# The last multiply-add of a conditioning set in PSUM writes the sum to SBUF, in place of a copy by ScalarE

## The chip, the core and the metric

The kernel runs on one core of a Trainium2 chip. The core has a matrix engine (TensorE, PE in the profile; its weight loads are PEld), a vector engine (VectorE, DVE), a scalar engine (ScalarE, ACT), a general engine (GpSimd, POOL) and a sync engine that issues most transfers (SyncE, SP). Each works through its own queue in order; they meet at semaphores. Data lies in SBUF; PSUM is the memory in which TensorE leaves its results. The metric is the device time of one execution in microseconds (us), the median of several runs.

## The reference

A trunk of two layers on 256 tokens of width 2048, in float32. Every sub-layer is normalized, scaled and shifted by a conditioning vector `mod`, and gated by it before the residual add. `mod` is what the change is about:

```python
c_act = jax.nn.silu(c)                       # c: 1 x 2048
for i in range(DEPTH):                       # 2 layers
    mod = c_act @ ada_w[i] + ada_b[i]        # ada_w[i]: 2048 x 12288
    sh1, sc1, g1, sh2, sc2, g2 = jnp.split(mod, N_MOD, axis=-1)
    h = modulate(rms_norm(x, norm_mix_g[i]), sh1, sc1)
    y = token_mixer(h)                       # layer 0: spatial gating; layer 1: attention
    x = x + g1[:, None, :] * y
    h = modulate(rms_norm(x, norm_ffn_g[i]), sh2, sc2)
    x = x + g2[:, None, :] * swiglu_ffn(h, ffn_w_gate[i], ffn_w_up[i], ffn_w_down[i])
return rms_norm(x, final_g)
```

## The kernel before

**Projections.** The large matrix products read weights in chunks of 1 MB (`wchunk`, L301): a load by SP into one of five `raw` buffers (L303), then for each half of the chunk a cast on ACT to a rounded `hi` (L290) and the remainder `lo` on DVE, for some chunks on POOL (L294). TensorE multiplies with `hi` and `lo` (L333 to L338, L351 to L353) into six PSUM banks tagged `mm`; two further banks, tagged `misc`, serve everything else. L735 adds a partial FFN product to its buffer on DVE, L481 adds a gated result to the residual, L547 adds to `v` of the first mixer.

**Conditioning.** `mod` is a vector times a matrix, 192 chunks of 1 MB in all. A *set* is 512 columns of one of the six parts in one layer, 4 chunks of 4 row blocks: 16 products. There are 48 sets. `pump` (L256) and `need` (L281) start chunks between those of the projections. Sets are summed in three ways:

- 11 sets on PE (`on_pe`, L164 to L173), copied out of PSUM at L195 into a tile `kept`.
- 31 sets on DVE with the sum in a `misc` bank (`in_bank[0]` true, `banked`): the first product at L178, 15 multiply-adds at L183. ACT then copies the sum to a tile `kept` in SBUF (L209).
- 6 sets on DVE during attention with the sum in SBUF (`in_bank[0]` false).

`kept` and the sums in SBUF share one ring of two buffers, `accp`. A sum of DVE still has 128 partial sums for each column, one in each partition: PE transposes it in four blocks (L214) into a `misc` bank, ACT sums each block along its rows (L217), and DVE adds the result to `mod` (L222).

**Order.** The framework's planner decides in which order instructions stand on each engine: `TileContext(nc, schedule_with_timeline_sim=True)` (L1050) runs the program against a timeline of its own and sets what is ready. A few orders are written out: `issue_after` keeps DVE's products behind a subtraction L294 that came earlier (L176).

**The first mixer**, layer 0, is where one place of the argument lies. After the last `v` product, `v_stats` (L617) makes the scale of the layer norm: ACT and DVE in `rsqrt` (L405 to L413), then L621 on DVE. `v_norm` (L625) applies it on ACT (L628), and the gating matmuls of `sgu` (L641) read the result.

Of the kernel before, what the change touches and what calls it, by code (L numbers as in the profile page):

```python
# [8 lines left out]
F32 = mybir.dt.float32  # L9
# [7 lines left out]
P = 128  # L17
D = 2048
T = 256
KT = D // P  # L20
# [13 lines left out]
def trunk_kernel(  # L34
# [24 lines left out]
    nc = tc.nc  # L59
# [6 lines left out]
    accp = ctx.enter_context(tc.tile_pool(name="accp", bufs=2))  # L66
# [6 lines left out]
    def misc():  # L73
        return psx.tile([P, 512], F32, tag="misc", name="misc")
# [24 lines left out]
    for i, v in enumerate((a_ln_g, a_ln_b)):  # L99
# [6 lines left out]
        out=fold[:, :32], in_=ident.rearrange("p (a j) -> p j a", a=4), axis=AX.X, op=ALU.add  # L106
# [8 lines left out]
    cact = const.tile([P, KT], F32, name="cact")  # L115
# [34 lines left out]
    def ada_chunk(layer, v, b0, q):  # L150

        raw = rawp.tile([P, 4, 512], F32, tag="raw", name="raw")
        nc.sync.dma_start(
            out=raw, in_=ada_v[layer][:, 4 * q : 4 * q + 4, v, P * b0 : P * b0 + 512]
        )
        if q == 0:
            ada_acc[0] = (
                misc() if in_bank[0] else accp.tile([P, 512], F32, tag="acc", name="acc"),
                in_bank[0],
            )  # L160
        acc, banked = ada_acc[0]
        for k in range(4):
            kt = 4 * q + k
            if (layer, v, b0) in on_pe:  # L164

                with ExitStack() as order:
                    if behind:
                        order.enter_context(tc.issue_after(behind[-1].ins))
                    nc.tensor.matmul(  # L169
                        acc[32 * k : 32 * k + 32, :], lhsT=cact32[:, kt, :], rhs=raw[:, k, :],  # L170
                        start=(q == 0), stop=(q == 3), skip_group_check=True,
                    )
                continue  # L173
            with ExitStack() as order:
                if paced:
                    order.enter_context(tc.issue_after(lo_last[-2].ins))  # L176
                if kt == 0:
                    nc.vector.tensor_scalar(  # L178
                        out=acc, in0=raw[:, k, :], scalar1=cact[:, 0:1], scalar2=None,
                        op0=ALU.mult,  # L180
                    )
                else:
                    nc.vector.scalar_tensor_tensor(  # L183
                        out=acc, in0=raw[:, k, :], scalar=cact[:, kt : kt + 1], in1=acc,
                        op0=ALU.mult, op1=ALU.add,
                    )
        if q == 3:
            ada_sum(layer, v, b0, acc, banked)

    def ada_sum(layer, v, b0, acc, banked):  # L190

        red = small.tile([P, 4], F32, tag="red", bufs=2, name="red")
        if (layer, v, b0) in on_pe:
            kept = accp.tile([P, 512], F32, tag="acc", name="kept")
            nc.scalar.copy(out=kept, in_=acc)  # L195
            pt = misc()
            for b in range(4):
                nc.tensor.matmul(
                    pt[:, b : b + 1], lhsT=kept[:, P * b : P * b + P], rhs=ones[:, 0:1],
                    start=True, stop=True,  # L200
                )
            nc.vector.tensor_add(
                out=mod[layer][:, 16 * v + b0 : 16 * v + b0 + 4],
                in0=pt[:, 0:4], in1=mod[layer][:, 16 * v + b0 : 16 * v + b0 + 4],
            )
            return ada_col(layer, v, b0)
        if banked:
            kept = accp.tile([P, 512], F32, tag="acc", name="kept")
            nc.scalar.copy(out=kept, in_=acc)  # L209
            acc = kept  # L210
        pt = misc()
        for b in range(4):
            bs = slice(P * b, P * b + P)
            nc.tensor.transpose(out=pt[:, bs], in_=acc[:, bs], identity=ident)  # L214
        for b in range(4):
            junk = tmp.tile([P, T], F32, tag="t", bufs=5, name="junk")
            nc.scalar.activation(  # L217
                out=junk[:, :P], in_=pt[:, P * b : P * b + P], func=AF.Identity,
                accum_out=red[:, b : b + 1],
            )  # L220
        dst = mod[layer][:, 16 * v + b0 : 16 * v + b0 + 4]
        nc.vector.tensor_add(out=dst, in0=dst, in1=red)  # L222
        ada_col(layer, v, b0)

    def ada_col(layer, v, b0):
        dst = mod[layer][:, 16 * v + b0 : 16 * v + b0 + 4]
        half, what = divmod(v, 3)
        if what == 1:
            s = slice(b0, b0 + 4)
            nc.vector.scalar_tensor_tensor(  # L230
                out=acol[layer][half][:, s], in0=dst, scalar=1.0,
                in1=(gain_mix, gain_ffn)[half][layer][:, s], op0=ALU.add, op1=ALU.mult,
            )
        ready.add((layer, v, b0))
# [17 lines left out]
    def ada_next():  # L252
        if ada_todo:
            ada_chunk(*ada_todo.pop(0))
# [247 lines left out]
    for t in range(NB):  # L502
        nc.scalar.activation(
            out=junk[:, D * t : D * t + D], in_=xt[t], func=AF.Square,
# [10 lines left out]
    for k in range(0, KT, 2):  # L515
        pt = misc()
        for b in range(2):
            for t in range(NB):
                nc.tensor.transpose(
                    out=pt[:, T * b + P * t : T * b + P * t + P],  # L520
                    in_=xt[t][:, P * (k + b) : P * (k + b) + P],
# [7 lines left out]
    v = [mgp.tile([P, D], F32, tag="mg", name="v") for _ in range(NB)]  # L529
# [36 lines left out]
    for k0, nk in ((0, 4), (4, 4), (8, 4), (12, 4)):  # L566
        if k0 == 4:
# [4 lines left out]
                out=pre[:, 0, :].rearrange("t (g s) -> t g s", s=P),  # L572
                in_=a_w_s[0].rearrange("g t s -> t g s"),
            )
            nc.sync.dma_start(
                out=pre[0:1, 1, :], in_=a_b_s[0:1].rearrange("o g t -> o (g t)")
# [3 lines left out]
                out=wst, in_=wst, pattern=[[0, 16], [-1, P]], compare_op=ALU.is_ge,  # L580
                fill=0.0, base=0, channel_multiplier=1,
            )
            for g0 in range(0, 16, 4):
                pt = misc()
                for g in range(4):
                    nc.tensor.transpose(
                        out=pt[:, P * g : P * g + P], in_=wst[:, g0 + g, :], identity=ident
# [9 lines left out]
                for g in range(4):  # L597
                    ps1 = slice(P * (g0 + g), P * (g0 + g) + P)
                    nc.vector.scalar_tensor_tensor(
                        out=pre[:, 1, ps1], in0=pt[:, P * g : P * g + P],  # L600
                        scalar=lnb_col[:, g0 + g : g0 + g + 1], in1=pre[:, 1, ps1],
# [328 lines left out]
    for g in range(4):  # L930
        qk = mgp.tile([P, 8, T], F32, tag="mg", name="qk")
        for w, (off, scale) in enumerate(((0, SCALE), (D, 1.0))):
# [5 lines left out]
            for j in range(4):  # L938
# [3 lines left out]
                    out=qk[:, 4 * w + j, :], in0=ps[j][:, 0:T], scalar=scale, in1=s,  # L942
# [8 lines left out]
            out=fb,  # L951
            in_=f_dram[4 * g : 4 * g + 4, :].rearrange("h t -> (h t)").partition_broadcast(P),
# [102 lines left out]
```

## Time and profile before

| | before |
|---|---|
| median of 3 runs | 2375.41 us (2370.2, 2375.41, 2375.45) |
| the profiled execution | 2370.1 us |
| its span, first to last instruction | 2368.4 us |
| mean granted clock of TensorE | 0.988 of full speed |
| instructions | 37510 |

The profile is that of one execution. *Busy* is the time in which an engine had an instruction running; the chain that ended last goes back from the last instruction, at each step to what released it. Matmuls are pipelined, so that PE's busy time is not PE at its peak. The trace gives each instruction's line, engine, operation, tiles (written `out<-in`), shape, start and duration.

### The profile page before, as it was taken

What the parts mean: (1) busy time and instruction counts of PE and PEld (TensorE: products, weight loads), DVE (VectorE), ACT (ScalarE), POOL (GpSimd) and SP (SyncE); (2) the same over time, 40 slices, a digit from 0 to 9 for tenths busy, and PEclk for the clock granted to TensorE, in tenths of its full rate; (3) what the DMA queues carried; (4) which work ended last, traced back from release to release, by engine and by line L of the source; (5) the groups of instructions that cost most, each with busy time, mean ns of one, the idle gap of its engine ahead of it and who ended that gap; (6) DMA issues with size and microseconds to landing.
All of it is one profiled execution on the core that took longest, in us unless ns stands there. A gap on an engine that the chain in (4) does not pass through costs nothing.

```text
span 2368.4 us, 37510 instructions
## 1 busy us (share of the span) xinstructions
PE 2293.4 (97%) x14837; PEld 2035.8 (86%) x14837; DVE 1632.0 (69%) x2382; ACT 1118.5 (47%) x1851; POOL 622.3 (26%) x379
## 2 busy tenths in 40 slices
PE   6999799999999999999999999999999999999998
PEld 3778678999988888888877888899999988888887
DVE  2356986789997777777797776677776844444564
ACT  4433644643554445544454554446444533444443
POOL 1323344444561112122211111220112411212221
PEclk8999899999999999999999999999999999999999
DMA  8878878998878788788787776689765555555552
GB/s 334 304 254 306 293 252 321 338 327 313 314 272 298 269 283 284 270 284 272 274 285 256 249 243 241 217 295 338 257 224 179 195 179 196 178 196 185 189 178 89
DMA packets 305043, 605.69 MB, mean 256 GB/s; under 512 B 11586, under 2 KB 11714, under 8 KB 304610
## 3 DMA queue, kind: packets, MB, share of 16 engines
q1 hardware_dynamic: 304578, 603.13, 73.0%
q8 instruction: 116, 1.90, 0.3%
q14 instruction: 59, 0.48, 0.1%
q0 software_dynamic: 288, 0.16, 0.0%
q10 hardware_dynamic: 2, 0.01, 0.0%
HBM read 601.15 MB, written 2.11 MB: 255 GB/s over the span
## 4 chain that ended last, share of the span: by engine, by line
PE 84%; DVE 9%; DMA 3%; ACT 2%; issue 1%; POOL 0%; SPq 0%; ACTq 0%; DVEq 0%
PE mm L333 31%; PE mm L338 25%; PE mm L336 9%; PE mm L335 9%; PE mm L351 2%; PE mm L352 2%; DVE misc L183 2%; PE mm L353 2%; DVE lo L294 2%; DMA raw<-in_a_w_in_dram 2%; PE misc L169 1%; ACT hi L290 1%; DVE gu L735 1%; DMA raw<-in_a_w_out_dram 1%; DVE m L440 1%
## 5 line engine op out<-in xcount | busy, mean ns | idle before, releaser
L290 ACT CAST hi<-raw 128x1024 fp32r<-128x1024 f32 x752 | 780.2, 1050 | 884.3 <-PE mm L333 493.6
L294 DVE TENSOR_TENSOR lo<-raw,hi 128x1024 fp32r<-128x1024 f32 x566 | 725.3, 1285 | 448.6 <-ACT hi L290 445.1
L338 PE MATMUL mm<-hA,lo 128*128 128x256 f32 x3584 | 983.1, 283 | 0.6 <-DVE lo L294 0.5
L294 POOL TENSOR_TENSOR lo<-raw,hi 128x1024 fp32r<-128x1024 f32 x186 | 471.2, 2534 | 1379.6 <-ACT hi L290 1305.6
L338 PEld LDWEIGHTS mm<-hA,lo 128*128 128x128 f32 x3584 | 681.2, 191 | 11.6 <-issue 1.1
L333 PE MATMUL mm<-hA,hi 128*128 128x512 f32 x1792 | 624.4, 398 | 8.4 <-DVE hA L458 4.5
L335 PE MATMUL mm<-hA,hi 128*128 128x256 f32 x1792 | 502.9, 285 | 7.3 <-DVE gu L735 5.6
L336 PE MATMUL mm<-hA,hi 128*128 128x256 f32 x1792 | 505.7, 284 | 0.5 <-DVE hA L458 0.5
L333 PE MATMUL mm<-m,hi 128*128 128x512 f32 x1248 | 432.7, 396 | 0.0
L333 PEld LDWEIGHTS mm<-hA,hi 128*128 128x128 f32 x1792 | 333.0, 189 | 80.2 <-DVE qk L941 4.6
L338 PE MATMUL mm<-m,lo 128*128 128x256 f32 x1408 | 383.1, 281 | 0.1
L335 PEld LDWEIGHTS mm<-hA,hi 128*128 128x128 f32 x1792 | 341.7, 192 | 16.8 <-DVE gu L735 7.6
L183 DVE SCALAR_TENSOR_TENSOR misc<-raw,cact,misc 128x512 f32<-128x512 f32 x465 | 348.2, 749 | 6.6 <-DMA raw<-in_ada_w_dram 1.0
L336 PEld LDWEIGHTS mm<-hA,hi 128*128 128x128 f32 x1792 | 344.9, 192 | 3.4 <-issue 2.4
L333 PEld LDWEIGHTS mm<-m,hi 128*128 128x128 f32 x1248 | 231.4, 188 | 49.7
L338 PEld LDWEIGHTS mm<-m,lo 128*128 128x128 f32 x1408 | 265.4, 189 | 5.6 <-DVE lo L294 0.3
L735 DVE TENSOR_TENSOR gu<-mm,gu 128x256 f32<-128x256 f32 x288 | 112.7, 415 | 52.4 <-PE mm L338 52.3
L481 DVE SCALAR_TENSOR_TENSOR xT<-mm,mod,xT 128x256 f32<-128x256 f32 x176 | 75.5, 477 | 54.1 <-PE mm L338 54.1
L351 PE MATMUL mm<-hi,hA 128*128 128x512 f32 x256 | 100.9, 401 | 3.1 <-ACT hA L453 3.1
L352 PE MATMUL mm<-lo,hA 128*128 128x512 f32 x256 | 101.6, 398 | 0.0
L353 PE MATMUL mm<-hi,hA 128*128 128x512 f32 x256 | 101.5, 398 | 0.0
L440 DVE TENSOR_TENSOR m<-mf,m 128x256 fp32r<-128x256 f32 x88 | 64.4, 743 | 14.2 <-ACT m L439 13.8
(211 smaller groups left out, 2090.8 us busy)
## 6 DMA issues: line engine op xcount, KB each, us to landing
raw<-in_ada_w_dram SPq DMA_DIRECT2D x192, 1024.0 KB, 6.0
raw<-in_ffn_w_gate_dram SPq DMA_DIRECT2D x88, 1024.0 KB, 5.4
raw<-in_ffn_w_up_dram SPq DMA_DIRECT2D x88, 1024.0 KB, 5.1
raw<-in_ffn_w_down_dram SPq DMA_DIRECT2D x88, 1024.0 KB, 5.0
raw<-in_b_w_in_dram SPq DMA_DIRECT2D x48, 1024.0 KB, 6.0
raw<-in_a_w_in_dram SPq DMA_DIRECT2D x32, 1024.0 KB, 6.9
raw<-in_a_w_out_dram SPq DMA_DIRECT2D x16, 1024.0 KB, 6.9
raw<-in_b_w_out_dram SPq DMA_DIRECT2D x16, 1024.0 KB, 5.7
```

The lines of the kernel that those rows point to most:

```text
L183: nc.vector.scalar_tensor_tensor(out=acc, in0=raw[:, k, :], scalar=cact[:, kt : kt + 1], in1=acc, op0=ALU.mult, op1=ALU.add,)
L290: nc.scalar.copy(out=out_hi, in_=src)
L294: ins = eng.tensor_sub(out=out_lo, in0=src, in1=out_hi.bitcast(F32))
L333: nc.tensor.matmul(ps[j], lhsT=hi[:, js], rhs=x, start=start, stop=False)
L335: nc.tensor.matmul(o, lhsT=hi[:, js], rhs=x[:, 0:T], start=start, stop=False)
L336: nc.tensor.matmul(o, lhsT=hi[:, js], rhs=x[:, T:], start=False, stop=False)
L338: nc.tensor.matmul(o, lhsT=lo[:, js], rhs=x[:, 0:T], start=False, stop=(kt == last))
L351: nc.tensor.matmul(ps[t], lhsT=xh, rhs=hi[:, k, :], start=(kt == first), stop=False)
L352: nc.tensor.matmul(ps[t], lhsT=xh, rhs=lo[:, k, :], start=False, stop=False)
L353: nc.tensor.matmul(ps[t], lhsT=xl, rhs=hi[:, k, :], start=False, stop=(kt == last))
L440: nc.vector.tensor_sub(out=dst[:, T:], in0=src, in1=dst[:, 0:T].bitcast(F32))
L735: nc.vector.tensor_add(out=dst, in0=ps[j][:, 0:T], in1=dst)
```

## The change

For a set whose sum lies in PSUM, the last of the 16 products (`kt == KT - 1`) takes a tile `kept` from the ring `accp` and writes there; its inputs stay the weights in SBUF and the sum in PSUM. The copy on ACT in `ada_sum` is gone, and the transposes read `kept` as before. The other two kinds of sets are as they were.

```diff
                 else:
+                    kept = acc
+                    if banked and kt == KT - 1:
+
+                        kept = accp.tile([P, 512], F32, tag="acc", name="kept")
                     nc.vector.scalar_tensor_tensor(
-                        out=acc, in0=raw[:, k, :], scalar=cact[:, kt : kt + 1], in1=acc,
+                        out=kept, in0=raw[:, k, :], scalar=cact[:, kt : kt + 1], in1=acc,
                         op0=ALU.mult, op1=ALU.add,
                     )
+                    acc = kept
         if q == 3:
-            ada_sum(layer, v, b0, acc, banked)
-
-    def ada_sum(layer, v, b0, acc, banked):
+            ada_sum(layer, v, b0, acc)
+
+    def ada_sum(layer, v, b0, acc):
...
-        if banked:
-            kept = accp.tile([P, 512], F32, tag="acc", name="kept")
-            nc.scalar.copy(out=kept, in_=acc)
-            acc = kept
         pt = misc()
```

## Rows read from the trace of the kernel before

**Rows 1.** The page's busy shares of the span, and its chain by engine
```profile
PE 2293.4 (97%) x14837; PEld 2035.8 (86%) x14837; DVE 1632.0 (69%) x2382; ACT 1118.5 (47%) x1851; POOL 622.3 (26%) x379
...
PE 84%; DVE 9%; DMA 3%; ACT 2%; issue 1%; POOL 0%; SPq 0%; ACTq 0%; DVEq 0%
```

**Rows 2.** Instructions of L209 and L214 (ns min/median/max, first and last start); DVE's wait
```profile
L209 ACT COPY kept<-misc x31: 567/586/592, 241.9 to 1729.0; 128x512 f32<-128x512 f32 x31
...
L214 PE MATMUL misc<-ident,kept x124: 270/272/477, 244.4 to 1738.2; 128*128 128x128 f32 x124
...
DVE misc L178 <- ACT kept L209: 1.5, 3, 1.0
```

**Rows 3.** Waits of PE: us in total, times, longest us
```profile
PE misc L214 <- ACT kept L209: 10.9, 3, 9.7
...
PE mm L333 <- ACT hi L290: 2.3, 2, 1.2
...
PE mm L335 <- ACT hi L290: 1.1, 3, 0.5
```

**Rows 4.** Timeline of 264.5 to 280: start, duration, engine, line [idle before <- releaser]
```profile
268.57 2.33 DVE L183 SCALAR_TENSOR_TENSOR misc<-raw,cact,misc 128x512 f32<-128x512 f32 x3
...
273.06 1.23 DVE L294 TENSOR_TENSOR lo<-raw,hi 128x1024 fp32r<-128x1024 f32 x1 [2.16 <-ACT hi L290]
273.88 0.58 ACT L209 COPY kept<-misc 128x512 f32<-128x512 f32 x1
...
274.49 0.76 DVE L178 TENSOR_SCALAR misc<-raw,cact 128x512 f32<-128x512 f32 x1 [0.21 <-ACT kept L209]
...
274.51 1.12 PE L214 MATMUL misc<-ident,kept 128*128 128x128 f32 x4 [9.67 <-ACT kept L209]
...
275.95 0.57 DVE L408 TENSOR_SCALAR nwt<-vmv 128x2 f32<-128x2 f32 x1
...
278.75 0.15 DVE L621 SCALAR_TENSOR_TENSOR vsh<-vmv,vrs 128x2 f32<-128x2 f32 x1
...
278.94 1.52 ACT L628 ACTIVATE v<-v,vsh,vrs 128x512 f32<-128x512 f32 x2 [2.13 <-DVE vsh L621]
...
279.80 0.58 PE L641 MATMUL mm<-pre,v 128*128 128x128 f32 x1 [4.17 <-ACT v L628]
```

**Rows 5.** Timeline at the two other places where PE waits for the copy
```profile
557.75 1.53 DVE L183 SCALAR_TENSOR_TENSOR misc<-raw,cact,misc 128x512 f32<-128x512 f32 x2
...
559.96 0.66 PE L214 MATMUL misc<-ident,kept 128*128 128x128 f32 x4 [0.61 <-ACT kept L209]
...
619.71 0.66 PE L214 MATMUL misc<-ident,kept 128*128 128x128 f32 x4 [0.61 <-ACT kept L209]
```

**Rows 6.** L209 in the stretch 540 to 690, and who waited for it
```profile
L209 ACT COPY kept<-misc x5: 581/586/589, 559.3 to 681.0; 128x512 f32<-128x512 f32 x5
...
  PE misc L214: 1.2, 2
```

**Rows 7.** Windows: stretch, us, busy (instructions) by engine, PEclk, DMA share, GB/s
```profile
core 0: us, PE busy (x) PEld busy (x) DVE busy (x) ACT busy (x) POOL busy (x), PEclk, DMA share, GB/s
264.80:279.80 15.00, 1.16 (x5) 0.72 (x5) 12.49 (x24) 9.90 (x22) 4.88 (x2) 0.64 0.82 280
279.80:300.00 20.20, 20.20 (x162) 20.20 (x163) 19.99 (x38) 14.13 (x26) 4.79 (x2) 0.93 0.80 266
540.00:690.00 150.00, 143.03 (x1172) 140.72 (x1172) 146.75 (x227) 72.11 (x132) 78.56 (x41) 1.00 0.85 299
```

**Rows 8.** DVE instructions by line: ns min/median/max, first and last start
```profile
L183 DVE SCALAR_TENSOR_TENSOR misc<-raw,cact,misc x465: 685/748/758, 213.0 to 1728.2; 128x512 f32<-128x512 f32 x155
...
L183 DVE SCALAR_TENSOR_TENSOR acc<-raw,cact,acc x90: 732/745/2951, 1185.3 to 1484.5; 128x512 f32<-128x512 f32 x90
...
L481 DVE SCALAR_TENSOR_TENSOR xT<-mm,mod,xT x176: 471/476/487, 323.6 to 2356.0; 128x256 f32<-128x256 f32 x176
...
L547 DVE TENSOR_TENSOR v<-mm,v x32: 668/690/692, 58.5 to 254.7; 128x512 f32<-128x512 f32 x32
...
L735 DVE TENSOR_TENSOR gu<-mm,gu x288: 403/414/426, 484.8 to 1883.4; 128x256 f32<-128x256 f32 x144
```

## Prediction, made before the changed kernel was run

> **What bounds the kernel now.** I read the page's busy shares first. TensorE (PE) is busy for 97% of the span and holds 84% of the chain that ended last; VectorE (DVE) holds 9% of it, ScalarE (ACT) 2% [rows 1]. So an edit pays only where PE stands still, or where DVE holds PE up. Next I read the line that goes: L209, the copy of a finished sum from PSUM to SBUF, runs 31 times at a median of 586 ns, 31 × 0.586 = 18.2 us of ACT, an engine that is busy for 47% of the span and holds 2% of the chain [rows 1, 2]. Third, PE's waits, which say what of those 18.2 us anyone waited for: PE stood idle for the copy in 3 of the 31 sets, 10.9 us in all, 9.7 of it in one; in the other 28 PE reached the transposes after the copy had ended [rows 2, 3]. Last, the timeline around those three places, for what else PE would have waited for.
>
> **What is removed.** 31 copies leave ACT and nothing takes their place there. The four transposes of a set (L214) wait for DVE's last multiply-add in place of ACT. A set's path gets shorter by one copy, 0.59 us, and by the time for which the copy stood in ACT's queue.
>
> *The wait of 9.7 us.* The last multiply-add of this set ends at 268.57 + 2.33 = 270.90. ACT has other work first, starts the copy at 273.88, and PE goes on at 274.51 [rows 4]. After the copy PE's transposes start about 0.05 us later (273.88 + 0.58 to 274.51), so with the change they start at 270.95, 3.56 us sooner. But the next thing on PE is the gating matmul of L641, which waits until 279.80 for ACT's normalization L628; that waits until 278.75 + 0.15 for L621 on DVE, the end of the statistics that begin at L408, 275.95 [rows 4]. DVE works in order there, and all of this stands behind the subtraction L294 at 273.06, which waited 2.16 us for its cast, and behind L178, the next set's first product [rows 4]. Of that chain the change shortens one link: L178 waited 0.21 us for the copy, because it takes the PSUM bank that the copy reads. So PE's wait for the copy falls to about 6.1 us and its wait for L628 grows from 4.17 to about 7.5: the second wait takes the place of the first. I count 0.21 us. The bounds are 0 (L178 finds another thing late) and 3.56 us (the statistics come as much sooner as the transposes).
>
> *The two waits of 0.61 us.* At 559.96 PE stands 0.61 us for the copy, and the multiply-add in front of it ended at 557.75 + 1.53 = 559.28; 619.71 is the same picture [rows 5]. Without the copy the transposes are ready at 559.33, while PE is finishing its last matmul. Both lie in the stretch 540 to 690, where PE is busy for 143.03 of 150 us [rows 7], so there is nothing else it would wait for just there. 2 × 0.61 = 1.22 us. The lower bound is 0: DVE is busy for 146.75 us of the same stretch [rows 7], with as much work as before, and PE may find it late at the next bank.
>
> *The other 28 copies* cost nothing: the transposes come later than the copy anyway, and what they hide behind is PE's own queue of matmuls. A cast (L290) that stood behind a copy comes 0.59 us sooner, but PE waited for casts for 2.3 + 1.1 = 3.4 us in the whole run [rows 3], so 0 to 3.4 us; I take 0, since five short waits can have met 31 copies by chance only, and all of ACT's work together holds 2% of the chain [rows 1]. DVE's waits for the copy, 1.5 us at L178 in 3 sets [rows 2], hold the 0.21 above; the other 1.3 us count from 0 to 1.3, and I take 0, since DVE is idle for 31% of the span [rows 1] and spends them elsewhere.
>
> **What is added.** No instruction. The last of 16 products of a set keeps its inputs (one tile in SBUF, the sum in PSUM) and writes SBUF instead of PSUM. The trace of before has this multiply-add in two forms: with the sum in PSUM throughout 748 ns, with the sum in SBUF throughout 745 [rows 8]. The mixed form at this size is not there. From the residual L481, a multiply-add that reads PSUM and writes SBUF at half the size, 476 ns, and from the step between two sizes of an add that reads PSUM, L547 less L735, 690 − 414 = 276 [rows 8], I estimate 752 ns; so −3 to +4 ns, 31 times: −0.1 to +0.1 us, counted as 0. One thing could make it dear: the form with both tensors in SBUF once took 2951 ns [rows 8], 2.2 us above its median. The adds and multiply-adds that read PSUM and write SBUF never went over 692 ns in 288 + 176 + 32 instructions, with POOL busy for 26% of the span [rows 1, 8]. The new form is one of these, so I exclude such stalls.
>
> [...]
>
> **What moves.** The SBUF buffer (two in the ring, shared with the sets that PE sums itself, L194) is taken at the last product instead of at the copy. So this DVE instruction now waits until PE has transposed the set two before it, with all of DVE's queue behind it: the next subtractions L294 and the products. The 31 copies begin between 241.9 and 1729.0, 30 steps of 50 us on average, and the transposes of the last begin by 1738.2, 9 us behind their copy [rows 2]; with two sets in between I count this wait at 0. If PE lay that far behind, it would cost DVE as much as PE is late. The PSUM bank comes free one copy sooner, for norms and transposes too. No DMA is moved: the last product still frees the weight buffer for SP's next load.
>
> **The sum.** 0.21 + 1.22 = 1.43 us. The profiled execution took 2370.1 us (span 2368.4 and 1.7 around it), so it would take 2368.7. The median of the runs is 2375.41, 5.3 above the profiled one, and the three runs themselves lie 5.2 apart; the median would be 2375.4 − 1.4 = 2374.0. With the bounds, 0 and 3.56 + 1.22 + 3.4 + 1.3 = 9.5, it lies between 2365.9 and 2375.4, most of it within the 0.3% (7.1 us) that a measurement of this kernel can tell from no change.
>
> **Rivals.** All of the sum takes the order on each engine as it is. But this order is the planner's (it runs the program against a timeline of its own), and 31 instructions and 31 waits leave that timeline.
>
> [...]
>
> *A new hole opens (slower).* PE's queue is in order. Without the copy the planner believes a sum ready sooner and may set its transposes further forward among the matmuls. Where DVE then runs behind the planner's timeline, PE stops, with everything behind it. This decides as soon as PE reaches the transposes before DVE's last product ends. Its price is that of the one such place in the trace: 9.67 us and 1.4 us of lower clock, 11.1; with the 1.4 gained, 2385.1. For it: DVE is busy for 98% of 540 to 690 [rows 7], five sets end there, and two of them already stop PE [rows 6]. Against it: 28 of 31 sets have no wait today, and the sum is really ready sooner, by more than the planner can believe where ACT's queue was long.
>
> *POOL stalls (slower).* If the write to SBUF made the last product wait for POOL as the form in SBUF once did, 2.2 us, the five sets of the stretch where DVE is busy throughout [rows 6, 7] would give up to 11 us: 2385. It decides as soon as POOL reads SBUF while the last product runs. Rows 8 speak against it.
>
> **Chances.** As summed, within 0.3%: 0.54. The hole closes wholly or for the greater part: 0.26. A new hole: 0.17. POOL: 0.03, half of which would still be seen as no change. So faster 0.26, same 0.55, slower 0.19. The range takes in both rivals at their price and a little beyond, 2358 to 2387; the likeliest case alone is 2366 to 2376.
>
> **What would show it.** Right: L209 gone and ACT's busy time lower by about 18 us; L183 at 465 in all, 434 of them into PSUM and 31 into SBUF at about 750 ns; at the second set PE waits about 6 us for DVE's L183 and about 7.5 for L628; the waits at the eleventh and thirteenth set gone; PE busy as before, near 2293. Wrong: transposes that wait for DVE in many sets, a different order of L641 and the projections on PE, or a last product of over 1 us.

## The result, and the profile after

The kernel after takes 2383.71 us, the median of runs from 2383.12 to 2387.14; the kernel before, measured beside it, 2373.43 (2370.2 to 2375.45). The ratio is 1.0052 with a 95% interval of [1.0041, 1.0063]: slower by 0.5%. The sum of the prediction said 1.4 us less than before; measured are 10.3 us more. The time lies inside its range of 2358 to 2387 all the same. The profiled execution of after took 2383.12 us, its span is 2381.1, 12.7 more than the span of before. Above L183 the lines are those of before; further down most numbers are one higher (L294 is now L295, L735 is L736), and the multiply-add is L187.

First the page of after, busy shares of the span and the chain by engine, to be read against [rows 1]:

```profile
PE 2296.8 (96%) x14837; PEld 2039.2 (86%) x14837; DVE 1657.2 (70%) x2382; ACT 1102.4 (46%) x1820; POOL 615.6 (26%) x379
...
PE 83%; DVE 11%; DMA 3%; issue 2%; ACT 1%; POOL 0%; SPq 0%; ACTq 0%; DVEq 0%
```

ACT does 16.1 us less (1118.5 to 1102.4), as wanted. DVE has the same 2382 instructions and is busy for 25.2 us longer (1632.0 to 1657.2), and its part of the chain rose from 9% to 11%. So the question is which of DVE's instructions got longer. It isn't the new one. Here are DVE's instructions of L187 in after (ns min/median/max, first and last start):

```profile
L187 DVE SCALAR_TENSOR_TENSOR misc<-raw,cact,misc x434: 684/749/759, 212.8 to 1739.6; 128x512 f32<-128x512 f32 x145
...
L187 DVE SCALAR_TENSOR_TENSOR kept<-raw,cact,misc x31: 731/748/749, 240.9 to 1741.0; 128x512 f32<-128x512 f32 x31
```

It takes 748 ns with a maximum of 749, against 748 for the form that it replaces [rows 8]. Where the time goes is found by following the same work in both traces. Between two fixed projection matmuls (the 2861st and the 4011th) lies the stretch that [rows 7] show: 540.1 to 690.1 before, 542.7 to 703.3 after. It begins 2.6 us late and ends 13.2 us late, and 10.6 of the 12.7 us arise in it. The 2.6 us at its start aren't explained; a run further down that has before's order on every compute engine up to there (ffn5) begins the stretch 2.2 us late as well. The window of the stretch in after (us, then busy time and instructions of PE, PEld, DVE, ACT and POOL, granted clock, DMA share, GB/s):

```profile
542.70:703.30 160.60, 146.87 (x1173) 142.84 (x1172) 158.72 (x227) 69.66 (x128) 76.36 (x41) 0.99 0.80 280
```

DVE runs 227 instructions in either kernel and needs 11.97 us more for them (158.72 against 146.75 over the same matmuls); the other half of DVE's 25.2 us lies outside, where the span grew by only 2.1 us. The groups of DVE in this stretch (busy us, mean ns, idle before) put the 11.97 on one line, L294 of before and L295 of after, with small shifts on others that nearly cancel; first before, then after:

```profile
L294 DVE TENSOR_TENSOR lo<-raw,hi 128x1024 fp32r<-128x1024 f32 x25 | 39.1, 1564 | 0.1
```

```profile
L295 DVE TENSOR_TENSOR lo<-raw,hi 128x1024 fp32r<-128x1024 f32 x25 | 51.3, 2052 | 0.0
```

The same 25 subtractions cost 12.2 us more. And PE's waits in this stretch (us in total, times, longest), first those of before for `gu`, then those of after:

```profile
PE mm L335 <- DVE gu L735: 5.6, 7, 1.3
```

```profile
PE mm L336 <- DVE gu L736: 12.5, 14, 2.1
PE misc L215 <- DVE kept L187: 1.3, 2, 0.6
```

Before, the wait for the copy was 1.2 us [rows 6]. So PE waits 7.0 us longer for DVE, and its 1173 matmuls take 3.84 us longer (143.03 to 146.87; the mean granted clock is 0.99 in place of 1.00, which is worth an estimated 1.5 us, 0.01 × 146.87; the rest of the 3.84 isn't explained). Together that is 10.8, where the stretch is 10.6 longer.

Why a subtraction of 1.2 us takes 3, the timeline shows. In before (start, duration, engine, line, in brackets the idle time ahead of it and what ended it):

```profile
553.68 2.40 POOL L294 TENSOR_TENSOR lo<-raw,hi 128x1024 fp32r<-128x1024 f32 x1 [5.78 <-ACT hi L290]
553.99 3.18 DVE L294 TENSOR_TENSOR lo<-raw,hi 128x1024 fp32r<-128x1024 f32 x1
...
559.32 0.59 ACT L209 COPY kept<-misc 128x512 f32<-128x512 f32 x1 [1.04 <-DVE misc L183]
559.53 1.21 DVE L294 TENSOR_TENSOR lo<-raw,hi 128x1024 fp32r<-128x1024 f32 x1
559.80 1.06 ACT L290 CAST hi<-raw 128x1024 fp32r<-128x1024 f32 x1
...
560.94 2.40 POOL L294 TENSOR_TENSOR lo<-raw,hi 128x1024 fp32r<-128x1024 f32 x1 [4.86 <-ACT hi L290]
560.99 0.74 DVE L178 TENSOR_SCALAR misc<-raw,cact 128x512 f32<-128x512 f32 x1
```

And in after, at the same set:

```profile
559.97 1.99 ACT L291 CAST hi<-raw 128x1024 fp32r<-128x1024 f32 x2 [3.89 <-DVE gu L736]
...
561.00 0.75 DVE L187 SCALAR_TENSOR_TENSOR kept<-raw,cact,misc 128x512 f32<-128x512 f32 x1
561.81 0.66 PE L215 MATMUL misc<-ident,kept 128*128 128x128 f32 x4 [0.63 <-DVE kept L187]
562.00 0.75 DVE L178 TENSOR_SCALAR misc<-raw,cact 128x512 f32<-128x512 f32 x1
562.04 2.40 POOL L295 TENSOR_TENSOR lo<-raw,hi 128x1024 fp32r<-128x1024 f32 x1 [3.48 <-ACT hi L291]
562.65 2.86 DVE L295 TENSOR_TENSOR lo<-raw,hi 128x1024 fp32r<-128x1024 f32 x1
```

Take the three pairs in turn. At 553.68 POOL's subtraction begins first, and DVE's, begun 0.31 us later, ends at 557.17, 1.09 us after POOL's end at 556.08. At 559.53 DVE's begins first, is done before POOL's next begins at 560.94, and takes 1.21 us. In after, at 562.65, POOL's has begun 0.61 us sooner; DVE's ends at 565.51, 1.07 us after POOL's end at 564.44. Both subtractions that started behind POOL's lasted until 1.07 to 1.09 us after its end, about the 1.21 us that one takes alone: as if they had stood still until POOL had done. L178 at 560.99 beside POOL's at 560.94 keeps its time (0.74 us), and so does the new multiply-add, which reads its sum from PSUM: 15 of the 31 in after begin while a TENSOR_TENSOR of POOL is running, and none takes over 749 ns. One tensor as input didn't spare every instruction: L1007, which reads and writes SBUF, begins at 2305.68 in before, 0.13 us behind a subtraction on POOL, and takes 2.43 us, the longest of its row (ns min/median/max):

```profile
L1007 DVE TENSOR_SCALAR fy<-xT,cols x32: 274/283/2434, 2270.7 to 2362.6; 128x128 f32<-128x128 f32 x32
```

It holds throughout: all subtractions of over 1.9 us in the stretch, 6 in before and 12 in after, end 1.07 to 1.09 us behind the end of one on POOL.

Two things differ between the two fences. The copy on ACT stopped ACT until DVE's last product was done (559.32) and stood 0.59 us in front of a cast; in after the two casts run one right behind the other, and POOL's subtraction starts 0.29 us behind the end of DVE's last product (561.75) in place of 1.66 (559.28, [rows 5]). And on DVE the next set's first product L178 needs the PSUM bank that the copy reads: in before it stands behind the subtraction (559.53, then 560.99), in after ahead of it (562.00, then 562.65), so that the subtraction is late by one product more. Subtractions of over 1.9 us in this stretch went from 6 to 12 of 25. The experiments take these two apart.

### The profile page after: what moved, and what is told of

Its sections match the earlier page's. It is cut to its first block, busy times and chain, and to the rows that moved or that the text cites. A ratio compares the mean times of both kernels' runs of the same rounds, so it can differ in the third digit from the quotient of the medians.

```text
span 2381.1 us, 37501 instructions
## 1 busy us (share of the span) xinstructions
PE 2296.8 (96%) x14837; PEld 2039.2 (86%) x14837; DVE 1657.2 (70%) x2382; ACT 1102.4 (46%) x1820; POOL 615.6 (26%) x379
## 4 chain that ended last, share of the span: by engine, by line
PE 83%; DVE 11%; DMA 3%; issue 2%; ACT 1%; POOL 0%; SPq 0%; ACTq 0%; DVEq 0%
PE mm L334 31%; PE mm L339 24%; PE mm L337 9%; PE mm L336 9%; DVE lo L295 3%; DVE misc L187 3%; PE mm L352 2%; PE mm L353 2%; PE mm L354 2%; PE misc L169 1%; DMA raw<-in_a_w_in_dram 1%; DVE gu L736 1%; DMA raw<-in_a_w_out_dram 1%; ACT hi L291 1%; DVE m L441 1%
## 5 line engine op out<-in xcount | busy, mean ns | idle before, releaser
L295 DVE TENSOR_TENSOR lo<-raw,hi 128x1024 fp32r<-128x1024 f32 x566 | 743.7, 1318 | 443.9 <-ACT hi L291 439.4
L295 POOL TENSOR_TENSOR lo<-raw,hi 128x1024 fp32r<-128x1024 f32 x186 | 464.6, 2498 | 1398.8 <-ACT hi L291 1361.1
L336 PE MATMUL mm<-hA,hi 128*128 128x256 f32 x1792 | 505.7, 287 | 14.1 <-DVE gu L736 12.5
L336 PEld LDWEIGHTS mm<-hA,hi 128*128 128x128 f32 x1792 | 342.9, 193 | 25.3 <-DVE gu L736 15.8
L187 DVE SCALAR_TENSOR_TENSOR misc<-raw,cact,misc 128x512 f32<-128x512 f32 x434 | 325.1, 749 | 5.3 <-DMA raw<-in_ada_w_dram 0.6
L736 DVE TENSOR_TENSOR gu<-mm,gu 128x256 f32<-128x256 f32 x288 | 113.3, 415 | 53.6 <-PE mm L339 53.4
```

The source lines that it names most:

```text
L187: nc.vector.scalar_tensor_tensor(out=kept, in0=raw[:, k, :], scalar=cact[:, kt : kt + 1], in1=acc, op0=ALU.mult, op1=ALU.add,)
L295: ins = eng.tensor_sub(out=out_lo, in0=src, in1=out_hi.bitcast(F32))
L336: nc.tensor.matmul(o, lhsT=hi[:, js], rhs=x[:, 0:T], start=start, stop=False)
L736: nc.vector.tensor_add(out=dst, in0=ps[j][:, 0:T], in1=dst)
```

## The experiments

The expectations name three explanations. *Port theory*: the lost time is that of DVE's subtractions that stand behind POOL's. *Write theory*: the new write to SBUF, or its wait for a buffer, costs something in each set. *Order theory*: the planner's other order costs time by itself, whatever POOL does.

**The loss has its place in five sets.** ffn5 makes the change for the sets 11 to 15 alone, those that end in the stretch; not5 makes it for the other 26.

```diff
+                    kept = acc
+                    if banked and kt == KT - 1:
+                        n_set[0] += 1
+                        if 11 <= n_set[0] <= 15:      # not5: if not 11 <= n_set[0] <= 15
+                            kept = accp.tile([P, 512], F32, tag="acc", name="kept")
+                            banked = False
```

> The change for 5 of the 31 sets alone, those that end in the stretch 540 to 690 of the kernel before; the other 26 keep the copy. Port theory: nearly the whole loss, +9 to +12 us, 2382-2386, with about 12 stalled subtractions in the stretch. Write theory, a cost for each set: 5/31 of 10 us, about 2375. Order theory: anything, but a change spread over the run rather than in the stretch.

> The other half: the change for 26 sets, the 5 that end in the stretch 540 to 690 keep the copy. Port theory: 2371-2377 (the sum of small gains and losses outside, about +2.7 by 410 us and some -1 to +2 later). Write theory: 26/31 of 10 us, about 2382.

Measured: ffn5 2381.84 us, ratio 1.0038 [1.0024, 1.0052]; not5 2372.56, 0.9997 [0.9987, 1.0007]. The subtractions on DVE in the stretch, ffn5 and then not5:

```profile
L302 DVE TENSOR_TENSOR lo<-raw,hi 128x1024 fp32r<-128x1024 f32 x25 | 51.3, 2053 | 0.0
```

```profile
L302 DVE TENSOR_TENSOR lo<-raw,hi 128x1024 fp32r<-128x1024 f32 x25 | 36.7, 1469 | 0.1
```

With 5 changed sets the stretch takes 160.5 us, as with all 31; with the other 26 it takes 149.4, and the whole kernel the time of before. ffn5 came out 0.2 us below the 2382 that were expected. So five sets carry the loss, and 26 instructions of the new form cost nothing that can be measured: the write theory is out. Of the subtractions in the stretch, 12 take over 1.9 us in ffn5 and 4 in not5.

**ACT's copy put back, with nothing depending on it.** dummy is after with a copy of the finished sum by ACT into a tile that nobody reads. It gives ACT's stop and its time back and leaves the bank free. tiny copies one column: the stop without most of the time.

```diff
+    dump = const.tile([P, 512], F32, name="dump")
...
+        if in_bank[0]:
+            nc.scalar.copy(out=dump, in_=acc)   # tiny: dump[:, 0:1], acc[:, 0:1]
         pt = misc()
```

> The changed kernel with a copy put back on ACT where the old one stood: it copies the finished sum from SBUF to a tile that nobody reads, 31 times, and the transposes don't wait for it. So ACT again stops until DVE's last product and is busy about 0.6 us. Port theory (the lost time is DVE's subtraction standing behind POOL's, because ACT and POOL run ahead of DVE without the copy): the stalls of L294's kind in the DVE-bound stretch fall from 12 to about 6, their busy time from 51 to about 39 us, and the time returns to 2370-2376, at best 1.2 us below before. Write theory (the new write or its wait for a buffer costs): stays at 2382-2386. Order theory (the planner's other order costs by itself, whatever POOL does): about 2371-2376 too, since the planner sees nearly the old load again; the runs with the subtractions off POOL tell that one apart.

> As the run before, but the copy that nobody reads has one column in place of 512: ACT still stops until DVE's last product, but is busy about 0.2 us only. If the stop is what holds ACT and POOL back (port theory, first form): 2370-2376, like the full copy. If the 0.59 us of ACT's time is what does it (port theory, second form): between the two, 2378-2385. Write theory: 2382-2386.

Measured: dummy 2380.22 us, 1.0028 [1.0017, 1.0039]; tiny 2381.94, 1.0038 [1.0026, 1.0051]. The stretch takes 157.6 and 158.2 us. The window and the subtractions in dummy:

```profile
539.70:697.30 157.60, 147.17 (x1172) 144.00 (x1172) 153.86 (x226) 71.96 (x132) 75.75 (x41) 0.98 0.81 284
...
L298 DVE TENSOR_TENSOR lo<-raw,hi 128x1024 fp32r<-128x1024 f32 x25 | 48.5, 1939 | 0.5 <-ACT hi L294 0.5
```

The expectation of dummy was missed: it was to come near before, and gave back 3.0 of the 10.6 us of the stretch. DVE's order in the stretch is nearly instruction by instruction that of after, so the 3.0 are ACT's part, its stop and its time, with one execution of each to go by. tiny gave back 2.4, which would put most of it on the stop; but its 2381.94 us also lie in the band that was expected if ACT's time were the cause, and two executions of after itself (160.6, and 161.8 in after2 below) lie 1.2 us apart there, so which of the two it is stays open. The timeline of dummy at the same set shows what stayed:

```profile
559.03 0.75 DVE L179 TENSOR_SCALAR misc<-raw,cact 128x512 f32<-128x512 f32 x1
...
559.68 1.21 DVE L298 TENSOR_TENSOR lo<-raw,hi 128x1024 fp32r<-128x1024 f32 x1
...
565.98 2.40 POOL L298 TENSOR_TENSOR lo<-raw,hi 128x1024 fp32r<-128x1024 f32 x1 [2.81 <-ACT hi L294]
566.03 3.44 DVE L298 TENSOR_TENSOR lo<-raw,hi 128x1024 fp32r<-128x1024 f32 x1
```

The first product (L179 here) is still ahead of the subtraction. POOL is held up enough to miss this one (its subtraction begins at 560.46, 0.78 us behind), and the next subtraction, begun 0.05 us behind POOL's, stands still for 2.2 us.

**The bank held as well.** dummyP has the new multiply-add, and ACT copies the PSUM bank (which nobody needs any more) behind it, so that the bank comes free as late as in before.

```diff
+                    if kept is not acc:
+                        rd = nc.scalar.copy(out=dump, in_=acc)
+                        tc.add_manual_dep(rd.ins, stt.ins.name, ...)   # behind the last product
```

> The changed kernel with a copy on ACT that nobody reads, this time of the PSUM bank after the last product. So ACT stops and is busy as in the kernel before, and besides the next set's first product has to wait for that bank again, so that the planner puts it behind a subtraction on DVE as before; the planned order on DVE in the stretch is then nearly that of before. What stays of the change is the write to SBUF and the transposes that wait for DVE. Port theory, with the order on DVE as its trigger: about 6 stalled subtractions in the stretch, 2370-2374, 0 to 1.4 us below before. Write theory: still 2380-2386. If ACT's copy alone were the trigger it would stay near the first copy run, 2380.

Measured: 2375.95 us, 1.0014 [1.0005, 1.0024]. The stretch takes 150.0 us, as in before; its window with the subtractions, and the order at the same set:

```profile
546.60:696.60 150.00, 143.65 (x1172) 140.90 (x1171) 143.02 (x226) 72.12 (x131) 79.26 (x41) 1.00 0.85 298
...
L305 DVE TENSOR_TENSOR lo<-raw,hi 128x1024 fp32r<-128x1024 f32 x25 | 36.4, 1454 | 0.1
```

```profile
564.75 0.59 ACT L193 COPY dump<-misc 128x512 f32<-128x512 f32 x1 [0.60 <-DVE kept L188]
564.96 1.22 DVE L305 TENSOR_TENSOR lo<-raw,hi 128x1024 fp32r<-128x1024 f32 x1
...
566.36 2.41 POOL L305 TENSOR_TENSOR lo<-raw,hi 128x1024 fp32r<-128x1024 f32 x1 [4.38 <-ACT hi L301]
566.43 0.75 DVE L179 TENSOR_SCALAR misc<-raw,cact 128x512 f32<-128x512 f32 x1
```

The order of before is back, subtraction first, and with it the time of the stretch. From after to dummy ACT's stop and time are worth 3.0 us, from dummy to dummyP the bank's release 7.6; what the bank would be worth without ACT's copy was not run. The whole kernel missed its expectation of 2370 to 2374. Its profiled execution is 6.5 us behind before where the stretch begins (546.6 against 540.1), nearly all of it by 410 us (PE's waits at the second set are 5.4 and 9.0, and the granted clock is 0.97 from 290 to 345 and 0.96 from 345 to 430, where before has 1.00 and 0.98); that part isn't explained.

**The collision taken away.** If the subtractions standing still are the cause, then a kernel in which POOL's subtraction waits for DVE's of the same chunk must lose nothing by the change. guard_a is after, guard_b before, with that wait in the first FFN only; guardall_a and guardall_b have it everywhere.

```diff
         if eng is nc.vector:
             lo_last.append(ins)
+        elif n_split[1] == 2 and paced and lo_last:   # guardall: elif lo_last:
+            tc.add_manual_dep(ins.ins, lo_last[-1].ins.name, ...)
```

> The changed kernel, and POOL's subtraction of a chunk now waits until DVE's subtraction of the same chunk has ended (in the FFN of layer 0 up to the end of its gate and up products). So no subtraction on DVE can start behind POOL's of its own chunk. Port theory: hardly any stalled subtraction in the stretch (0 to 2 in place of 12), its busy time near 25 x 1.22 = 31 us in place of 51; the time falls by 10 to 20 us, to 2364-2374, unless POOL's later end makes TensorE wait for its half. Order theory (PE's and DVE's other order costs by itself): 2380-2385 whatever POOL does.

> The same wait of POOL in the kernel before. Port theory: its 6 stalled subtractions go too, 31 us in place of 39; 2364-2374, and the difference to the changed kernel with the same wait is within 4 us, in place of 10. Order theory: the difference stays near 10 us.

Measured: guard_a 2372.39 us, 0.9997 [0.9987, 1.0007]; guard_b 2367.82, 0.9980 [0.9972, 0.9989]. The window and the subtractions on DVE in the stretch, guard_a and then guard_b:

```profile
540.60:687.20 146.60, 142.22 (x1172) 140.54 (x1171) 140.74 (x229) 69.50 (x127) 75.57 (x42) 1.00 0.87 308
...
L295 DVE TENSOR_TENSOR lo<-raw,hi 128x1024 fp32r<-128x1024 f32 x25 | 31.5, 1259 | 0.5 <-ACT hi L291 0.4
```

```profile
541.10:685.50 144.40, 141.58 (x1172) 140.47 (x1171) 138.76 (x227) 72.88 (x132) 75.18 (x41) 1.00 0.88 312
...
L294 DVE TENSOR_TENSOR lo<-raw,hi 128x1024 fp32r<-128x1024 f32 x25 | 31.7, 1267 | 1.0 <-ACT hi L290 0.8
```

The subtractions take 1.26 and 1.27 us each, and the stretch 146.6 and 144.4 us: with the wait the changed kernel falls from 160.6 to below the 150.0 of before. In guard_b the order on all five engines is that of before, instruction by instruction, so its 5.3 us are POOL's wait and nothing else. In guard_a DVE's order is still that of after through most of the stretch, the next set's first product ahead of the subtraction; so of the 10.6 us at most the 2.2 that are left between the two windows can be that order's own. As long as POOL waits, DVE runs first:

```profile
547.41 2.41 POOL L294 TENSOR_TENSOR lo<-raw,hi 128x1024 fp32r<-128x1024 f32 x1 [1.31 <-DVE lo L294]
...
552.17 1.22 DVE L294 TENSOR_TENSOR lo<-raw,hi 128x1024 fp32r<-128x1024 f32 x1
...
553.62 2.41 POOL L294 TENSOR_TENSOR lo<-raw,hi 128x1024 fp32r<-128x1024 f32 x1 [3.81 <-DVE lo L294]
```

There remained 4.6 us between guard_a and guard_b, a little over the 4 that were expected. In after there are such collisions outside the first FFN too:

```profile
377.31 2.36 POOL L295 TENSOR_TENSOR lo<-raw,hi 128x1024 fp32r<-128x1024 f32 x1 [2.51 <-ACT hi L291]
377.72 3.02 DVE L295 TENSOR_TENSOR lo<-raw,hi 128x1024 fp32r<-128x1024 f32 x1
...
380.80 0.44 PE L339 MATMUL mm<-yB,lo 128*128 128x256 f32 x1 [2.33 <-DVE lo L295]
```

The last three runs are after once more (after2), and the wait everywhere in both kernels.

> The changed kernel as it is, timed side by side with the kernel before on the chip of the runs around it: 1.004 to 1.006 of before, 2382-2387, if the loss is the kernel's and not one chip's.

> The kernel before with POOL's wait for DVE's last subtraction everywhere, not only in the first FFN. Unlike the run with the wait in the first FFN alone, the planned order changes too. Port theory: outside the first FFN TensorE hides most of DVE's stalls, so little more to gain: 2363-2370, within 4 us of the run with the wait in one place; if POOL's later halves make TensorE wait, a few us worse.

> The same wait everywhere in the changed kernel. Port theory: 2364-2373, again 10 us or more below the changed kernel without it; the difference to the kernel before with the same wait within 5 us.

Measured: after 2384.39 us, 1.0048 [1.0031, 1.0064]; guardall_b 2365.67, 0.9968 [0.9957, 0.9980]; guardall_a 2363.08, 0.9966 [0.9953, 0.9979]. With the wait everywhere the change costs nothing that can be measured (the intervals lie on each other; guardall_a came out 0.9 us below the 2364 that were expected), and without it 0.5%. Both are faster than either kernel of the comparison. That the 4.6 us came from collisions elsewhere would fit with their vanishing here, but it isn't shown: the profiled executions of guard_a and guard_b have spans of 2365.8 and 2365.4, and what they do show is the 2.2 us in the stretch itself, where the subtractions take the same time in both.

## Why the prediction was wrong, point by point

**The new instruction: right.** Costed at nothing, from an estimate of 752 ns; it took 748 in 31 instructions, against 748 of the form in PSUM. The form in SBUF took 745 [rows 8], 3 less. That it wouldn't stand behind POOL held as well: maximum 749 ns, with 15 of the 31 begun while a TENSOR_TENSOR of POOL was running.

**The ring of `kept`: right.** No wait of DVE for a free buffer: what DVE sat idle for ahead of its L187 was 0.6 us for two loads.

**The hole at the second set: right, to half a microsecond.** Forecast were waits of about 6.1 us for the sum and 7.5 for the normalization. In after, the timeline shows:

```profile
269.56 0.75 DVE L187 SCALAR_TENSOR_TENSOR kept<-raw,cact,misc 128x512 f32<-128x512 f32 x1
...
270.37 1.12 PE L215 MATMUL misc<-ident,kept 128*128 128x128 f32 x4 [5.58 <-DVE kept L187]
...
278.20 0.15 DVE L622 SCALAR_TENSOR_TENSOR vsh<-vmv,vrs 128x2 f32<-128x2 f32 x1
...
279.25 1.22 PE L642 MATMUL mm<-pre,v 128*128 128x128 f32 x4 [7.77 <-ACT v L629]
```

The waits were 5.58 and 7.77 us, 13.35 in place of 13.84 [rows 4]: as said, the second wait took over what the first gave up. So the hole did not close, a case to which the prediction gave 0.26; the lower end of its range, 2358, is the price of that case, and no run shows it: the two waits fell by 0.49 us.

**The two waits of 0.61 us: wrong in size.** Those of [rows 5] were to go, 1.22 us. Two waits of 0.6 stand in the stretch as before, now for DVE (0.63 at 561.81, in the fence above): the transposes are reached by PE just before the sum is ready. The lower bound of the prediction, 0, named the reason, DVE late at the next place.

**"A cast (L290) that stood behind a copy comes 0.59 us sooner ... I take 0", and "The PSUM bank comes free one copy sooner", at no price: here the prediction failed, and in the sign.** The cast was bounded by what PE waits for casts, 0 to 3.4 us of gain, as if a cast that is ready sooner could only help. A cast releases a subtraction, some of them on POOL, and with POOL sooner more of DVE's stood behind it: 12 of over 1.9 us in the stretch in place of 6. dummy puts ACT's stop and its time at 3.0 us of loss in the stretch. The bank is the larger part, and failed in the same way: a resource that comes free sooner was counted as no loss. The planner set the next set's first product ahead of a subtraction on DVE, which then began behind POOL's, and from dummy to dummyP that is 7.6 us. The reasons given for 0 were averages over the run (ACT at 2% of the chain, DVE idle for 31% of the span), and the loss lies in a stretch where DVE is idle for 2%.

**The rival with POOL: right mechanism, wrong instruction.** The prediction looked for stalls behind POOL at the changed instruction, found that its form has none, and gave the case 0.03. The form that has them is L294, which the change doesn't touch and which stood in [rows 4] only as something to wait for. Its mean in the stretch (1564 ns, with a duration of 1.23 in [rows 4]) would have shown that 8.8 us of standing still were there already: 39.1 less 25 × 1.21. How much an edit could make of that can be bounded from before's trace as well: 25 subtractions, each some 2.2 us at most (the longest of L294, 3.44, less 1.21), in a stretch in which DVE is busy for 98% [rows 7].

**The rival of a new hole**, at 2385.1, came within 1.4 us of the time, by luck. It named the right stretch, but its mechanism is another: PE hardly stops at the transposes (1.3 us in 2 places, as before), and instead at L336, which waits for the partial products `gu`, in 14 short places, 2.1 us at the longest in place of one of 9.67. No run shows the 1.4 us of lower clock in its 11.1 us: that was the author's estimate, (1 − 0.93) × 20.2, from the clock granted behind the hole in before [rows 7]. What the runs show is the granted clock itself: in the 20.2 us behind the hole in after, from 279.25, it was 0.85, and in the stretch where the loss lies 0.99. It is luck, too, that the time lies in the range.

## What to carry to other kernels

Where instructions of two engines stand still for each other, as those of DVE and POOL do here, an edit to a third engine can change which of them goes first (here 12 subtractions took over 1.9 us in the stretch, in place of 6): look, in the stretch where one of them is busy throughout, at the forms whose mean lies far above their median, and ask of each edit what it does to the start of both. "Sooner" is a gain only for the thing that is needed next; a cast that comes sooner or a bank that comes free sooner can change what runs ahead of what, as the two did here for 3.0 and 7.6 us of loss, and gets a price with both signs. Where DVE is the bound and POOL has time, let POOL's half wait for DVE's: here it was worth 0.2% in one stage and 0.3% everywhere, and with it everywhere the change no longer showed in the time.

## What the runs showed of the hardware

A subtraction of two SBUF tensors of 128x1024 on DVE took 1.21 us alone (before, at 559.53) and 2.86 to 3.44 us where POOL's of the same size (2.36 to 2.40 us) had begun 0.05 to 0.61 us ahead: in the four such pairs that are shown (two in after, one each in before and dummy) it ended 1.07 to 1.09 us after POOL's end. In the stretch where DVE is busy throughout this cost 8.8 us in before and 21.0 (51.3 less 25 × 1.21) in after, while a multiply-add of 128x512 took 748 ns with its sum read from PSUM, whether it wrote PSUM or SBUF. POOL's waited too where it came second: in after a subtraction on DVE began at 583.96 and took 1.22 us, and POOL's, begun 0.04 us behind it, took 3.43 in place of 2.40.
